# The last two feed-forward tiles as seven block products, two of them held over, and the modulation jobs distributed anew

## The chip, the cores and the metric

The kernel runs on one core of a Trainium2 chip. The metric is the device time of one execution in microseconds (us), lower is better. A run is one execution; a profiled execution also leaves a trace.

## The reference

One inference step of a two-layer backbone over 640 tokens (512 latent, 128 context) of width 1024. Each layer is a half-step SwiGLU feed-forward, a token mixer (layer 0 a Fourier mixer, layer 1 a 16-head attention), and another half-step feed-forward. Each sub-layer has a norm before and after it, with shift, scale and gate from a modulation of the conditioning vectors.

```python
def _half_ffn(x, m, k, g_pre, g_post, w1, w2):
    h = _rmsnorm(x, g_pre) * (1 + m[:, 3 * k + 1, None]) + m[:, 3 * k, None]
    gate, up = jnp.split(h @ w1, 2, axis=-1)          # w1: 1024 x 5632
    y = (jax.nn.silu(gate) * up) @ w2                 # w2: 2816 x 1024
    return x + 0.5 * m[:, 3 * k + 2, None] * _rmsnorm(y, g_post)

def _modulation(cond, w_mod, b_mod):                  # w_mod: 1024 x 9216 per layer
    return (jax.nn.silu(cond) @ w_mod + b_mod).reshape(cond.shape[0], 9, D_MODEL)
```

All of it is float32.

## The kernel before

**Layout.** Activations lie transposed: 1024 channels as 8 chunks of 128 partitions, the 640 tokens along the free axis in two halves of 320. Every fp32 product is made of three float32r matmuls (`mm3`, L203 to L208): a high part times a high part, high times low, low times high. `split` (L200 ACT, L201 DVE) makes the two parts of an activation, L190 (ACT) and L191 (DVE) those of a weight.

**Units.** All weights pass through one list of units of 128x1024 (`list_units`). `unit(i)` sends units up to i + 3: a 512 KB DMA on SP's queue into one of 4 raw buffers (`raw`), then L190 and L191 into one of 6 pairs of weight buffers, or, for a "block", into two blocks of a ring of 20 (`ring`), which also holds activations.

**Sub-layers.** n = 0 to 5: feed-forward, Fourier, feed-forward, feed-forward, attention, feed-forward. In the text "layers 0, 2, 3, 5" are the feed-forward ones by this n. Each ends half 0 with `boundary`, which starts a chain of steps for that half: the post norm, the residual, the next pre norm (`post`, `pre`). The chain of half 0 runs on DVE and ACT while PE still works on half 1; the next sub-layer's first matmuls need its result.

**A feed-forward layer** has 22 f tiles of 128 (NF = 22). A tile needs gate and up, each over 8 chunks and 2 halves. Tiles 0 to 3 are done plainly. Tiles 4 to 19 (`FAST`) go through `w1_fast`, a Strassen-Winograd scheme: gate and up against the lower and upper 4 chunks and the two halves of the tokens make a 2x2 block product, done as seven products of 4 chunks each, on sums of weights (L175 to L183, units gate, sums, up, all) and sums of activations (`combine`). Products go to banks x, y, z, w; DVE and ACT add between them (L587 to L609); `hidden` splits the result into g[f]. The second products (`w2`) run by slices of f tiles; slice s adds to `y` through a seed (L621) and a copy back (L633). Slices 0 to 3 are woven between the fast tiles, 16 steps each. Tiles 20 and 21 are done plainly by `late` after the fast ones: both for half 0, then 20 for half 1; 21 for half 1 comes after half 0's second products of the last slice, as cover for half 0's chain. `late` reuses the first 4 chunks' sum of half 0 for half 1, which it copies out of the half-summed bank (L539).

**Modulation jobs.** 128 jobs (`behind`): each loads 512 KB of w_mod into a raw buffer and does two multiply-and-sum operations on DVE (`gemv`, L336). `BEHIND` spreads them over a feed-forward layer's second products; the Fourier and attention code calls `behind` at places of its own. The whole order of instructions on each engine is fixed when the program is built, by a list scheduler that goes by priority and by its own estimate of what is ready; `high_priority` moves an instruction forward there.

Of the kernel before, what the change touches and what calls it, by code (L numbers as in the profile page):

```python
# [42 lines left out]
FAST = range(4, NF - 2)  # L43
BEHIND = (28, 20, 28, 28, 24, 0)
# [64 lines left out]
class Kernel:  # L109
    def __init__(self, ctx, tc, io, subs=6):  # L110
# [23 lines left out]
        self.fast = {}  # L134
# [29 lines left out]
    def send(self, kind, src):  # L164


        nc, two, one = self.nc, slice(512, UNIT), slice(0, 512)
# [23 lines left out]
        nc.vector.tensor_tensor(lo, raw[:, at], hi.bitcast(F32), op=ALU.subtract)  # L191
        return hi, lo
# [288 lines left out]
    def ffn(self, layer, which, base, boundary):  # L481
# [12 lines left out]
        def w1(fs, half):  # L494
# [4 lines left out]
            if fs[0] >= NF - 2:  # L499
                pss = [late(fs[0], j, half) for j in range(2)]  # L500
            elif len(fs) == 1:
# [5 lines left out]
            for i, f in enumerate(fs):  # L507
                gate, up = pss[2 * i], pss[2 * i + 1]
                s, v = self.temp("left"), self.temp("right")
                with self.tc.high_priority():  # L510
                    if f in kept and half:
                        for j, (to, ps) in enumerate(((s, gate), (v, up))):
                            nc.vector.tensor_tensor(to[:, :HALF], ps[:, :HALF], kept[f][j], op=ALU.add)
                        nc.scalar.activation(s[:, :HALF], s[:, :HALF], AF.Silu)
                        nc.vector.tensor_tensor(v[:, :HALF], v[:, :HALF], s[:, :HALF], op=ALU.mult)
                    else:
                        nc.scalar.activation(s[:, :HALF], gate[:, :HALF], AF.Silu)
                        nc.vector.tensor_tensor(v[:, :HALF], up[:, :HALF], s[:, :HALF], op=ALU.mult)  # L518
# [4 lines left out]
        def late(f, j, half):  # L523


            if f not in kept:
                if not kept:
                    kept["room"] = quad(self.ring(F32))
                a = 2 * (f - NF + 2)
                kept[f] = [kept["room"][:, a + i, :] for i in range(2)]  # L530
            w = self.unit(base + self.w1_at[f] + j)
            ps = self.bank()
            for k in range(NCH):
                x = part(1, k) if half and k < 4 else self.h.chunk(k, half)
                self.mm3(ps[:, :HALF], w[0][:, k * P : (k + 1) * P], w[1][:, k * P : (k + 1) * P], *x,
                         k == 0, k == NCH - 1 or (k == 3 and not half), k > 3 and not half)
                if k == 3 and not half:
                    with self.tc.high_priority():
                        nc.scalar.activation(kept[f][j], ps[:, :HALF], AF.Copy)  # L539
            return ps  # L540
# [27 lines left out]

        def w1_fast(f):
            g[f] = self.ring(F32R).rearrange("p (a t) -> p a t", a=2)  # L570
            u = base + self.w1_at[f]

            def product(ps, unit, at, x, start):
                w = self.unit(u + unit)
                for k in range(4):
                    a = at + k * P
                    self.mm3(ps[:, :HALF], w[0][:, a : a + P], w[1][:, a : a + P], *x(k), start and k == 0, k == 3, not start)

            tt = nc.vector.tensor_tensor
            a, q = (self.temp("left")[:, :HALF] for _ in range(2))  # L580
            s, v = (self.temp("right")[:, :HALF] for _ in range(2))
            px, py, pz, pw = self.bank(), self.bank("score"), self.bank(), self.bank()
# [694 lines left out]
```

## Time and profile before

| what | value |
|---|---|
| median of 3 runs | 2336.14 us (2333.36 to 2336.28) |
| profiled execution | 2334.2 us |
| its span, first to last instruction | 2332.4 us |
| mean granted TensorE clock | 0.993 |
| PE matmul / weight load busy | 98% / 95% |
| DVE / ACT busy | 72% / 54% |
| matmuls | 15756 |
| DMA moved | 278.13 MB, mean 119 GB/s |

A busy share is an average over stages with different limits; matmuls are pipelined, so the durations of single ones overlap, and how many start in a stretch says more than their sum. DVE is VectorE, ACT ScalarE, PE TensorE, SP the engine that issues the DMAs. A name such as `main<-ring,hi` reads: output tile from input tiles, buffer numbers left out.

### The profile page before, as it was taken

The page shows a single profiled execution, that of the slowest core. Times are in us where ns is not written, and L with a number is a line of the kernel's source. Part 1 is how long each engine was busy: PE and PEld are TensorE (multiplying, and loading weights), DVE is VectorE, ACT ScalarE, POOL GpSimd, SP SyncE. Part 2 cuts the span into 40 slices and gives each one's busy share as a digit, 9 for nine tenths or more (in the row PEclk, how much of TensorE's full clock was granted, in tenths as well). Part 3 has the DMA queues.
Part 4 walks back from the last instruction along what each step waited for, and adds up shares of the span by engine and source line. Part 5 has one row for each costly group of instructions (what it writes and reads, how often), then busy time and mean ns, then how long its engine had stood idle before and what let it go on. Part 6 is the DMA issues. An engine that isn't in the chain of part 4 may idle for free.

```text
span 2332.4 us, 39397 instructions
## 1 busy us (share of the span) xinstructions
PE 2278.2 (98%) x15756; PEld 2225.2 (95%) x15756; DVE 1686.6 (72%) x2934; ACT 1270.9 (54%) x2448; POOL 45.4 (2%) x64
## 2 busy tenths in 40 slices
PE   6999999998999999999999999999999999999997
PEld 4999999997999999999999999998888899999997
DVE  4878877389788877847878887378877485765553
ACT  4445545564653545556545555567767664545554
POOL 0000000000000000000000000010000000000000
PEclk9999999999999999999999999999999999999998
DMA  8234434334423433443234434224543212221241
GB/s 300 82 115 139 145 118 136 109 103 153 146 99 112 152 109 127 136 154 109 82 125 129 145 118 144 101 81 149 162 135 106 86 73 82 93 89 64 82 136 46
DMA packets 80280, 278.13 MB, mean 119 GB/s; under 512 B 8800, under 2 KB 15200, under 8 KB 79968
## 3 DMA queue, kind: packets, MB, share of 16 engines
q1 hardware_dynamic: 79824, 275.29, 36.1%
q8 instruction: 123, 2.02, 0.4%
q14 instruction: 61, 0.50, 0.1%
q10 hardware_dynamic: 272, 0.33, 0.0%
HBM read 264.04 MB, written 11.53 MB: 118 GB/s over the span
## 4 chain that ended last, share of the span: by engine, by line
PE 88%; DVE 5%; ACT 3%; DMA 3%; issue 1%; POOL 0%; SPq 0%; DVEq 0%; ACTq 0%; POOLq 0%
PE main L206 25%; PE main L208 25%; PE main L207 25%; PE score L206 3%; PE score L208 3%; PE score L207 3%; DVE junk L336 1%; PE sum L1108 1%; PE turn L1092 1%; PE sum L419 1%; DVE lo L191 1%; ACT hi L190 1%; PE score L1066 1%; DMA first<-in_w_mod_k 1%; DMA raw<-in_w_mod_t 1%
## 5 line engine op out<-in xcount | busy, mean ns | idle before, releaser
L206 PE MATMUL main<-ring,hi 128*128 128x320 f32 x3872 | 1204.5, 312 | 3.9 <-ACT ring L200 2.9
L208 PE MATMUL main<-ring,lo 128*128 128x320 f32 x3872 | 1198.0, 310 | 1.6 <-DVE lo L191 1.6
L207 PE MATMUL main<-ring,hi 128*128 128x320 f32 x3872 | 1198.9, 310 | 0.2 <-DVE ring L201 0.2
L206 PEld LDWEIGHTS main<-ring,hi 128*128 128x128 f32 x3872 | 727.7, 188 | 10.0 <-ACT ring L200 3.8
L208 PEld LDWEIGHTS main<-ring,lo 128*128 128x128 f32 x3872 | 727.6, 188 | 2.2 <-DVE lo L191 1.9
L207 PEld LDWEIGHTS main<-ring,hi 128*128 128x128 f32 x3872 | 728.1, 188 | 1.4 <-DVE ring L201 0.9
L190 ACT ACTIVATE hi<-raw 128x1024 fp32r<-128x1024 f32 (+1 forms) x358 | 350.3, 981 | 457.7 <-PE main L207 384.2
L191 DVE TENSOR_TENSOR lo<-raw,hi 128x1024 fp32r<-128x1024 f32 (+1 forms) x358 | 402.6, 1126 | 153.7 <-ACT hi L190 152.5
L336 DVE SCALAR_TENSOR_TENSOR junk<-raw,wide 128x1024 bf16<-128x1024 f32 x256 | 312.4, 1220 | 21.2 <-DMA raw<-in_w_mod_t 18.6
L633 ACT ACTIVATE y<-main 128x320 f32<-128x320 f32 x320 | 138.5, 433 | 172.3 <-PE main L208 170.9
L372 DVE TENSOR_TENSOR total<-total,square 128x640 f32<-128x640 f32 x71 | 58.3, 823 | 108.0 <-ACT square L371 106.1
L621 ACT ACTIVATE main<-y 128x320 f32<-128x320 f32 x256 | 111.9, 439 | 27.2 <-DVE left L607 10.5
L206 PE MATMUL score<-ring,hi 128*128 128x320 f32 x384 | 118.8, 309 | 0.0
L207 PE MATMUL score<-ring,hi 128*128 128x320 f32 x384 | 118.7, 309 | 0.0
L208 PE MATMUL score<-ring,lo 128*128 128x320 f32 x384 | 118.7, 309 | 0.0
L191 DVE TENSOR_TENSOR lo<-sums,hi 128x1024 fp32r<-128x1024 f32 x64 | 78.1, 1221 | 51.1 <-ACT hi L190 51.1
L206 PE MATMUL main<-ring,ring 128*128 128x320 f32 x352 | 110.5, 315 | 0.0
L208 PE MATMUL main<-ring,ring 128*128 128x320 f32 x352 | 108.9, 309 | 0.0
L207 PE MATMUL main<-ring,ring 128*128 128x320 f32 x352 | 108.7, 309 | 0.0
L190 ACT ACTIVATE hi<-sums 128x1024 fp32r<-128x1024 f32 x64 | 67.9, 1061 | 26.4 <-PE main L207 20.5
L200 ACT ACTIVATE ring<-right 128x320 fp32r<-128x320 f32 x112 | 51.6, 467 | 50.6 <-DVE right L518 40.6
L593 DVE TENSOR_TENSOR left<-left,main 128x320 f32<-128x320 f32 x64 | 31.2, 487 | 60.6 <-PE main L208 60.6
(181 smaller groups left out, 2676.1 us busy)
## 6 DMA issues: line engine op xcount, KB each, us to landing
raw<-in_w SPq DMA_DIRECT2D x264, 512.0 KB, 3.6
raw<-in_w_mod_t SPq DMA_DIRECT2D x128, 512.0 KB, 3.7
raw<-in_qkv SPq DMA_DIRECT2D x26, 512.0 KB, 3.7
first<-in_w_mod_k SPq DMA_DIRECT2D x16, 512.0 KB, 8.7
spill<-ring SPq DMA_DIRECT2D x12, 640.0 KB, 3.6
ring<-spill SPq DMA_DIRECT2D x12, 640.0 KB, 4.8
raw<-in_bias SPq DMA_DIRECT2D x16, 448.0 KB, 3.7
raw<-in_four_in SPq DMA_DIRECT2D x8, 512.0 KB, 3.5
```

Source lines behind the costliest of these rows:

```text
L190: nc.scalar.activation(hi, raw[:, at], AF.Copy)
L191: nc.vector.tensor_tensor(lo, raw[:, at], hi.bitcast(F32), op=ALU.subtract)
L200: self.nc.scalar.activation(hi, src, AF.Copy)
L206: mm(out, whi, xhi, start=start, stop=False)
L207: mm(out, whi, xlo, start=False, stop=False)
L208: self.latest = mm(out, wlo, xhi, start=False, stop=stop)
L336: last = self.nc.vector.scalar_tensor_tensor(out=self.junk, in0=raw, scalar=1.0, in1=self.wide[:, cond, :], op0=ALU.mult, op1=ALU.mult, ac ...
L372: nc.vector.tensor_tensor(acc, acc, sq, op=ALU.add)
L419: self.spread = nc.tensor.matmul(ps[:, t : t + P], col[:, j : j + 1].to_broadcast([P, P]), self.ident, start=True, stop=True)
L593: tt(a, q, z, op=ALU.subtract)
L621: nc.scalar.activation(ps[:, :HALF], self.y[:, m, lo:hi], AF.Copy)
L633: nc.scalar.activation(self.y[:, m, lo:hi], ps[:, :HALF], AF.Copy)
```

## The change

`FAST` now reaches to tile 21, and `late` goes. Tiles 20 and 21 (`LATE`) run as five of their seven products in `w1_fast`, which give half 0 whole; the partial sums a and q of half 1 stay in two temporaries. The other two products (`one`, `two`, on bank w) are `tail`, and both tails stand between half 0's and half 1's second products of the last slice. Their weights are one more unit, "mix", whose 1024 columns are the sum that was "up" and the difference that was "all"; it is built in place in the raw tile by "u2" and stays in that raw buffer until "mix" splits it into ring blocks. The jobs per sub-layer n go from 28, 20, 28, 28, 24, 0 to 36, 12, 28, 32, 12, 8: in a feed-forward layer they now also follow half 0's second products of the last slice (but for n = 5); in the Fourier layer three follow each fold of half 1, none lies among the groups of `positions`, and six stay in the output projection; in attention every third step has one.

```diff
-FAST = range(4, NF - 2)
-BEHIND = (28, 20, 28, 28, 24, 0)
+FAST = range(4, NF)
+LATE = (NF - 2, NF - 1)
+BEHIND = (36, 12, 28, 32, 12, 8)
...
-        elif kind == "up":
+        elif kind in ("up", "u2"):
             raw = self.fast["up"]
+            at = at if kind == "up" else two
+        elif kind == "mix":
+            raw = self.mixed.pop(0)
...
-        if kind == "block":
+        if kind in ("block", "mix"):
             hi, lo = (self.ring(F32R)[:, :n] for _ in range(2))
...
+        if kind == "u2":
+            nc.vector.scalar_tensor_tensor(out=raw[:, two], in0=self.fast["sums"][:, two], scalar=-1.0,
+                                           in1=self.fast["gate"][:, two], op0=ALU.mult, op1=ALU.subtract)
+            self.mixed.append(raw)
...
         def w1_fast(f):
...
-            product(pw, 2, 0, lambda k: part(1, k), True)
-            with high():
-                tt(a, a, w, op=ALU.add)
-            product(px, 0, 512, lambda k: self.h.chunk(4 + k, 0), False)
+            if not late:
+                w = one(f, a, 2)
+            product(f, x, 0, 512, lambda k: self.h.chunk(4 + k, 0), False)
             with high():
                 nc.scalar.activation(s, x, AF.Silu)
-            product(pz, 2, 512, lambda k: part(4, k), False)
+            product(f, z, 2, 0 if late else 512, lambda k: part(4, k), False)
             with high():
                 tt(v, q, z, op=ALU.subtract)
                 tt(v, v, s, op=ALU.mult)
                 hidden(f, v, 0)
-            product(pw, 3, 0, lambda k: self.h.chunk(4 + k, 1), False)
+            if late:
+                kept[f] = a, q
+            else:
+                two(f, a, q, w, 3, 0)
+
+        def one(f, a, unit):
+            w = self.bank()[:, :HALF]
+            product(f, w, unit, 0, lambda k: part(1, k), True)
+            with high():
+                tt(a, a, w, op=ALU.add)
+            return w
+
+        def two(f, a, q, w, unit, at):
+            product(f, w, unit, at, lambda k: self.h.chunk(4 + k, 1), False)
             with high():
                 nc.vector.scalar_tensor_tensor(out=q, in0=w, scalar=-1.0, in1=q, op0=ALU.mult, op1=ALU.subtract)
                 nc.scalar.activation(q, q, AF.Silu)
                 tt(a, a, q, op=ALU.mult)
                 hidden(f, a, 1)
+
+        def tail(f):
+            a, q = kept[f]
+            mix = self.mix_at[f] - self.w1_at[f]
+            two(f, a, q, one(f, a, mix), mix, 512)
...
-                if a[0] < len(SLICES) - 1:
+                if a[0] < len(SLICES) - 1 or half == 0:
                     passed += 1
-                    due = BEHIND[n] * passed // (2 * NCH * (len(SLICES) - 1))
+                    due = min(BEHIND[n], BEHIND[n] * passed // (2 * NCH * (len(SLICES) - 1) + (NCH if n < 5 else 0)))
...
-        a, b = NF - 2, NF - 1
-        plan += [("w1", (a,), 0), ("w1", (b,), 0), ("w1", (a,), 1), ("x", None, None)]
+        plan += [("x", None, None)]
         for half in (0, 1):
             if half == 1:
-                plan += [("w1", (b,), half)]
+                plan += [("tail", f, None) for f in LATE]
             plan += [("w2", (due, m), half) for m in range(NCH)]
             plan += [("end", None, half)]
...
-                self.ffn_units += [("gate", v, 0), ("sums", v, 1), ("up", None, None), ("all", None, None)]
+                self.ffn_units += [("gate", v, 0), ("sums", v, 1)]
+                self.ffn_units += [(kind, None, None) for kind in (("u2",) if v in LATE else ("up", "all"))]
+            elif op == "tail":
+                self.mix_at[v] = len(self.ffn_units)
+                self.ffn_units += [("mix", None, None)]
...
                 if half:
                     fold(m0, nc.vector)
-                self.behind(2)
+                    self.behind(3)
...
             positions(g)
-            if g < 6:
-                self.behind()
...
-            if n < 35 and (n % 5 < 3 or n in (3, 8, 13)):
+            if n < 35 and n % 3 == 0:
                 parts.append(self.behind)
```

## Rows read from the trace of the kernel before

**Rows 1.** The page: busy time of each engine (part 1).

```profile
PE 2278.2 (98%) x15756; PEld 2225.2 (95%) x15756; DVE 1686.6 (72%) x2934; ACT 1270.9 (54%) x2448; POOL 45.4 (2%) x64
```

**Rows 2.** Busy time by stretch, feed-forward stretches; columns in the first line.

```profile
core 0: us, PE busy (x) PEld busy (x) DVE busy (x) ACT busy (x) POOL busy (x), PEclk, DMA share, GB/s
160.00:200.00 40.00, 40.00 (x275) 40.00 (x274) 34.24 (x61) 21.95 (x39) 0.00 (x0) 1.00 0.40 132
2000.00:2040.00 40.00, 40.00 (x274) 40.00 (x274) 26.39 (x41) 23.36 (x44) 0.00 (x0) 1.00 0.30 98
```

**Rows 3.** Busy time by stretch, the last two f tiles, layer 0.

```profile
394.00:436.00 42.00, 41.66 (x281) 40.99 (x280) 22.70 (x34) 20.61 (x36) 0.00 (x0) 1.00 0.62 204
436.00:456.00 20.00, 20.00 (x139) 20.00 (x138) 2.96 (x4) 12.03 (x24) 0.00 (x0) 1.00 0.05 17
```

**Rows 4.** Busy time by stretch, the Fourier layer's groups and their end.

```profile
550.00:580.00 30.00, 21.81 (x166) 19.80 (x167) 29.63 (x75) 14.77 (x33) 0.00 (x0) 0.91 0.32 102
575.00:580.00 5.00, 3.06 (x15) 2.77 (x15) 5.00 (x12) 1.33 (x4) 0.00 (x0) 0.50 0.43 142
```

**Rows 5.** Busy time by stretch, attention: the sum of six stretches, 1600 to 1840.

```profile
sum 240.00, PE 233.07 PEld 207.72 DVE 180.72 ACT 177.60 POOL 8.81; mean PE 38.85 PEld 34.62 DVE 30.12 ACT 29.60 POOL 1.47
```

**Rows 6.** Busy time by stretch, from half 0's end to half 1's, layer 0.

```profile
455.00:483.50 28.50, 28.50 (x200) 28.31 (x199) 21.85 (x33) 21.15 (x46) 1.70 (x2) 1.00 0.26 82
```

**Rows 7.** Timeline of DVE: start, duration (us); next layer's first low part.

```profile
481.67 0.82 DVE L201 TENSOR_TENSOR ring<-y,ring 128x640 fp32r<-128x640 f32 x1
```

**Rows 8.** Groups by line, 361 to 410: count, busy us, mean ns, idle before.

```profile
L191 DVE TENSOR_TENSOR lo<-raw,hi 128x1024 fp32r<-128x1024 f32 x9 | 11.0, 1222 | 3.7 <-ACT hi L190 3.7
L190 ACT ACTIVATE hi<-raw 128x1024 fp32r<-128x1024 f32 x9 | 9.5, 1061 | 13.8 <-PE main L207 9.9 <-DMA raw<-in_w 3.0 <-ACT right L599 0.9
...
L176 DVE TENSOR_TENSOR raw<-raw 128x512 f32<-128x512 f32 x2 | 1.4, 692 | 0.1
...
L607 DVE SCALAR_TENSOR_TENSOR left<-main,left 128x320 f32<-128x320 f32 x2 | 1.0, 484 | 0.0
```

**Rows 9.** Timeline, tile 19's SiLU in half 1; tile 20's multiply and low part.

```profile
411.35 0.47 ACT L608 ACTIVATE left<-left 128x320 f32<-128x320 f32 x1 [0.38 <-DVE left L607]
...
417.99 0.49 DVE L518 TENSOR_TENSOR right<-main,left 128x320 f32<-128x320 f32 x1 [2.06 <-PE main L208]
419.02 0.49 DVE L201 TENSOR_TENSOR ring<-right,ring 128x320 fp32r<-128x320 f32 x1 [0.54 <-ACT ring L200]
```

**Rows 10.** Line 539, copies of a half-summed bank: durations, who waited.

```profile
L539 ACT ACTIVATE ring<-main x16: 413/434/438, 413.6 to 2257.2; 128x320 f32<-128x320 f32 x16
...
  PEld main L206: 3.6, 12
  PE main L206: 0.8, 3
```

**Rows 11.** DMA issues by line: count, KB each, median us to landing.

```profile
raw<-in_w SPq DMA_DIRECT2D x264, 512.0 KB, 3.6
...
ring<-spill SPq DMA_DIRECT2D x12, 640.0 KB, 4.8
```

**Rows 12.** Line 336 (a job's gemv), last layer: DVE busy (count), clock, DMA.

```profile
1850.00:2290.00 440.00, 0.00 (x0) 1.00 0.26 87
```

**Rows 13.** Timeline of DVE, one Fourier group, from L855 to L855.

```profile
560.69 0.33 DVE L855 SCALAR_TENSOR_TENSOR ring<-main,col,ring 128x128 fp32r<-128x128 f32 x1
560.95 1.21 DVE L336 SCALAR_TENSOR_TENSOR junk<-raw,wide 128x1024 bf16<-128x1024 f32 x1
...
562.69 1.21 DVE L336 SCALAR_TENSOR_TENSOR junk<-raw,wide 128x1024 bf16<-128x1024 f32 x1
...
565.23 0.33 DVE L855 SCALAR_TENSOR_TENSOR ring<-main,col,ring 128x128 fp32r<-128x128 f32 x1
```

**Rows 14.** Waits, 1560 to 1845: us in total, times, longest.

```profile
PEld turn L1092 <- ACT right L1094: 10.3, 22, 1.4
...
PE turn L1092 <- ACT right L1094: 5.0, 11, 1.2
```

More of the change, by code (lines that the diff above doesn't have):

```diff
@@ L498, in w1 @@
             pss = []
-            if fs[0] >= NF - 2:
-                pss = [late(fs[0], j, half) for j in range(2)]
-            elif len(fs) == 1:
+            if len(fs) == 1:
                 for j in range(2):
@@ L510, in w1 @@
                 with self.tc.high_priority():
[L511 to L518, printed above, removed]
+                    nc.scalar.activation(s[:, :HALF], gate[:, :HALF], AF.Silu)
+                    nc.vector.tensor_tensor(v[:, :HALF], up[:, :HALF], s[:, :HALF], op=ALU.mult)
                     hidden(f, v, half)
@@ L521, in w1 @@
                     self.later.pop()()
[L523 to L540, printed above, removed]
         def part(i, k):
@@ L567, in combine, with product @@
                 self.split(sums[i][0][:, k : k + 2, :], sums[i][1][:, k : k + 2, :], to)
+        high, tt = self.tc.high_priority, nc.vector.tensor_tensor
+        def product(f, ps, unit, at, x, start):
+            w = self.unit(base + self.w1_at[f] + unit)
+            for k in range(4):
+                a = at + k * P
+                self.mm3(ps, w[0][:, a : a + P], w[1][:, a : a + P], *x(k), start and k == 0, k == 3, not start)
         def w1_fast(f):
             g[f] = self.ring(F32R).rearrange("p (a t) -> p a t", a=2)
-            u = base + self.w1_at[f]
@@ L573, in product @@
[L573 to L579, printed above, removed]
+            late = f in LATE
             a, q = (self.temp("left")[:, :HALF] for _ in range(2))
             s, v = (self.temp("right")[:, :HALF] for _ in range(2))
-            px, py, pz, pw = self.bank(), self.bank("score"), self.bank(), self.bank()
@@ L583, in w1_fast @@
-            x, y, z, w = (ps[:, :HALF] for ps in (px, py, pz, pw))
-            high = self.tc.high_priority
-            product(px, 0, 0, lambda k: self.h.chunk(k, 0), True)
+            x, y, z = (self.bank(kind)[:, :HALF] for kind in ("main", "score", "main"))
+            product(f, x, 0, 0, lambda k: self.h.chunk(k, 0), True)
             with high():
                 nc.scalar.activation(a, x, AF.Copy)
-            product(py, 1, 512, lambda k: part(2, k), True)
+            product(f, y, 1, 512, lambda k: part(2, k), True)
@@ L589, in w1_fast @@
             with high():
                 tt(q, y, a, op=ALU.subtract)
-            product(pz, 1, 0, lambda k: part(3, k), True)
+            product(f, z, 1, 0, lambda k: part(3, k), True)
             with high():
                 tt(a, q, z, op=ALU.subtract)
-            product(pw, 2, 0, lambda k: part(1, k), True)
-            with high():
-                tt(a, a, w, op=ALU.add)
-            product(px, 0, 512, lambda k: self.h.chunk(4 + k, 0), False)
+            if not late:
+                w = one(f, a, 2)
@@ L721, in list_units @@
                         elif op == "w1":
-                            self.units.append(("block" if v in (3, NF - 1) else "plain", io["w1"][i, sub // 2, v, j]))
+                            self.units.append(("block" if v == 3 else "plain", io["w1"][i, sub // 2, v, j]))
                         else:
```

6 lines of the change are left out of this document (4 added, 2 removed).

## The prediction

> **What bounds the kernel now.** I read the page's totals first, then the busy table in stretches of 40 us, then the waits inside the stretches where TensorE (PE) isn't full, and last the queues of the engines that feed it. The totals [rows 1] put matmuls at 98% of the span and VectorE (DVE) at 72%. In the feed-forward layers PE is full for hundreds of us: 40.00 of 40 us, 274.5 matmuls, in the densest stretch beside 34.24 us of DVE [rows 2]. That gives 40 / 274.5 = 0.1457 us for one 128x128x320 matmul, and there a removed matmul is worth its whole time. PE isn't full in three places: the last two f tiles of a feed-forward layer, a little [rows 3]; the groups of the Fourier layer, where DVE is busy 29.63 of 30 us and PE 21.81 [rows 4]; and the attention layer [rows 5].
>
> **The products.** Two f tiles in plain form are 2 tiles x 2 (gate, up) x 8 k x 2 halves x 3 matmuls = 192. As seven block products they are 2 x 7 x 4 x 3 = 168. 24 matmuls fewer in each of four layers: 96 x 0.1457 = 14.0 us off a full PE. 120 of the 168 come before half 0's second products (144 before the change) and 48 after them (48 before), so what covers half 0's norm chain stays 48 + 144 matmuls. That chain has its first chunk's low part at 481.67 + 0.82 = 482.5 us, while PE is busy without a gap up to 483.5 [rows 6, 7]: about 1 us of room.
>
> **New work on DVE and ACT.** Each late f tile is split as gate 1024, sums 1024, u2 512 and mix 1024 columns instead of 2048: 1536 columns more, 1.5 x 1.06 = 1.6 us of ACT and 1.5 x 1.22 = 1.8 us of DVE, and four 512-wide sums or differences of 0.69 = 2.8 us of DVE [rows 8]. For two tiles that is about 9 us of DVE, beside 4 more modulation jobs of 2.4 us in half 0's second products in layers 0, 2 and 3. Now DVE works 22.70 of 42 us and then 2.96 of 20 in this place [rows 3]: 25.7 + 9 + 9.8 = 44.5 of 62 - 3.5 us. The sum fits, so I charge no time for the amount, only for the order. Four places, each per layer:
> (a) Half 0. Tile 21 now ends with a product, and the second products need its result as their sixth tile, 5 x 3 x 0.1457 = 2.2 us later. Behind the product stand a subtraction (0.5), then multiply, high part and low part: multiply to low part takes from 417.99 to 419.02 + 0.49, 1.5 us [rows 9]. 2.0 us and the hand-over against 2.2: nothing if DVE is free, 1.2 if a 1024-wide split stands in the way. I take 0.3.
> (b) Half 1, behind the second tail: a negating subtraction 0.48 [rows 8], SiLU 0.47 [rows 9], then the same 1.5, so 2.5 and hand-overs, 0.3 to 0.5 late; up to 1.7 if an operation of the norm chain goes first. Taken: 0.5.
> (c) In a tail, product six is read by DVE out of the bank that product seven adds to, so PE must wait for that read unless other matmuls stand between. Nearest row: the old code copies a half-summed bank in the same way, 16 times, and PE waited 0.8 us for all 16 (its weight loads 3.6) [rows 10]: 0.05 each where the order leaves room. The other end is a read with nothing between, 0.49 and two hand-overs, about 0.9. Two tails a layer: 0.1 to 1.8; taken 0.4, less the 0.2 of the copies that go.
> (d) Load buffers. There are four; the raw tiles of both late f tiles stay in two of them from u2 to mix, so the six second-product units and two of the jobs must pass through the other two. One pass takes 3.6 us landing [rows 11] + 1.06 high + 1.22 low [rows 8] = 5.9. Eight through two buffers: 4 x 5.9 = 23.6 us, from about 1 us into tile 21's products (60 x 0.1457 = 8.7 us long) to the use of the sixth unit, 40 x 3 x 0.1457 = 17.5 us into the second products, 26.2 in all. Room of 1.6 us. Each us of landing beyond that room takes 4 us, and the four reloads of x (640 KB, landing 4.8 [rows 11]) now crowd into this stretch. At 4.8 the layer would lose 3.2. I take 0.6 for layers 0, 2, 3; layer 5 has no jobs here and takes 0.
> Sum: 0.3 + 0.5 + 0.2 + 0.6 = 1.6 in three layers, 1.0 in the last: 5.8. Bounds: -0.8 (only the copies go) to some 28 (1.2 + 1.7 + 1.8 + 3.2 in each of three layers, 4.7 in the fourth). Feed-forward net: 14.0 - 5.8 = 8.2 gained.
>
> On (c), the Trainium skill's "TensorE: Matmul & The Clock Gate", section "Part 2: What happens when you issue a matmul", speaks against the change: only weight loads are pulled ahead, "the MATMULs themselves stay in program order". By it alone the two products of a tail stand still at the read, which is rival 2. The row of the sixteen copies disagrees only if the written order put other matmuls between, which no row here names.
>
> **Modulation.** Jobs per layer go from 28, 20, 28, 28, 24, 0 to 36, 12, 28, 32, 12, 8. Layer 0's first four slices get 32 instead of 28: 9.8 us of DVE over some 300 us, 1.3 per 40, where the densest row has 34.24 [rows 2]. PE's cover holds until DVE is full; cost 0, and if the jobs bunch, some 2 us. Layer 5 gets 8 where DVE works 26.39 of 40 [rows 2] and had none [rows 12]: 0.
> Fourier: the six jobs among the groups go. A group now takes 565.23 - 560.69 = 4.54 us, with two 1.21 us gemv operations in it [rows 13]; without them DVE needs 2.1 to 2.2, and PE's own 21.81 / (30 / 4.54) = 3.3 us sets the pace. PE's idle 8.2 us of the 30 can go. The granted clock is 0.50 in the last 5 of them, behind the gaps [rows 4], that is 1.2 instead of 2.4 GHz: half of 3.06 busy us more, 9.7 in all. Against this stand six jobs behind the projections of half 1 (four stood there): two more, 4.9 us of DVE, run on into the first groups, and PE's slack over DVE there is about 1.1 a group, so some 2.7 are lost. Net 7.0. Ends: 9.7, and 9.7 - 7.3 = 2.4 if the three jobs behind the second fold stand in front of the first group's splits. The four jobs that leave half 0's projections free DVE where PE loses under 1 us: 0.
> Attention: 24 jobs to 12, 29 us less of DVE's 180.72 in 240 [rows 5]. But PE waits there for ACT copies (5.0 us) [rows 14], which a job delays only through what ACT waits for. Bounds 0 to 7 (7 is what PE isn't busy there); taken 1.5, near the lower end, as the row names ACT.
> Weight loads wait 10.3 us for those copies [rows 14]; if half of that goes with the jobs, attention gives 5, the figure of the high rival.
> By the Trainium skill's "Perfetto Trace Analysis", section "Identifying the Most-Contended Engine", weight-load time, not matmul time, measures PE's headroom: 207.72 of 240 instead of 233.07 [rows 5]. By it there is room for more than 5; no row here says that DVE stands behind it.
>
> **Sum.** 8.2 + 7.0 + 1.5 = 16.7. The profiled execution took 2334.2 us (span 2332.4 and 1.8 around it), 1.9 below the median of the runs shown, 2336.14. 2334.2 - 16.7 = 2317.5; I write 2318, as the runs lie a little above the profile.
>
> **Rivals.**
> 1. Everything is hidden: 14.0 - 0.5, Fourier 9.7, attention 5: 2334.2 - 28.2 = 2306. For it: PE lost only 0.34 us in the whole stretch of the old late tiles [rows 3]. Against it: DVE has twice the work there. Chance 0.2.
> 2. The tails stand still: 0.9 at each of 8 reads instead of 0.2, and (b) at 1.2: 5.6 + 2.8 more, 2326. For it: the two products of a tail are written one behind the other. Against: the copies' 0.05. Chance 0.14.
> 3. Slower: the load buffers. If a landing takes 5.9 us in half 0's second products, eight passes take 4 x 8.2 + 1 = 33.8 us, 7.6 late in each of layers 0, 2, 3; with (d) at 0 the rest gains 18.5, so about here the sum passes +0.2%. At 6.5 us: 9.9 x 3 = 29.8, 2345. For it: 6 units, jobs and 2.6 MB of x in 20 us where the DMA engines now carry nearly nothing [rows 3]. Against: x lands in 4.8 even now, with loads in front of it. Chance 0.07.
> 4. Nothing much moves: landings of 5 us (4 late in three layers, 10 more than summed) and the Fourier jobs only shifted (2.4): 2332. Chance 0.08.
>
> **Numbers.** The forecast has 0.51, in 2311 to 2324. A measurement of this kernel can tell about 0.2% (4.7 us) from no change: below 2331.4 is faster. Forecast, rivals 1 and 2 and a little of 4 give 0.86 for faster, 0.07 for the same, 0.07 for slower. The range takes in rival 1's time and rival 2's and leaves out the worst of 1, the upper part of 4 and 3: 2305 to 2329.
>
> **What would show it.** 15660 matmuls, 96 fewer, if no records are missing. In the stretch of the last two f tiles: PE gaps of 0.3 to 0.6 at the low part of the last tile (a, b), at the tail's read (c); and gaps at a second-product unit's high or low part whose ACT operation waited for a DMA (d). In the Fourier groups: a period near 3.3 us, the clock at full, DVE below 25 of 30. In attention DVE lower, PE's wait for ACT copies nearly as before. The prediction is wrong if PE's waits in the late tiles exceed 3.5 us a layer, if the six jobs turn up among the Fourier groups, or if PE falls behind in layer 0's slices.

## The result, and the profile after

The change takes 2321.2 us (median of 4 runs, 2319.2 to 2323.81) against 2336.21 (4 runs, 2333.36 to 2336.65): ratio 0.9939, 95% interval 0.9922 to 0.9956, some 15 us less. The profiled execution took 2319.2 us, span 2317.4; the one before took 2334.2. So profile against profile gives 15.0, where 16.7 was forecast.

The page's totals of the kernel after (before: [rows 1]):

```profile
PE 2260.0 (98%) x15660; PEld 2209.5 (95%) x15660; DVE 1731.6 (75%) x3006; ACT 1275.8 (55%) x2456; POOL 46.5 (2%) x64
```

There are 96 matmuls fewer. Line numbers have shifted: the three matmuls are now L215 to L217 (were L206 to L208), a weight's high and low part L195 and L196 (L190, L191), an activation's L209 and L210 (L200, L201), a job's gemv L345 (L336).

Busy time by stretch, after: three stretches of the last two f tiles and half 0's end in layer 0 (columns as in [rows 2]; they answer to [rows 3, 6]), the Fourier groups, and their end [rows 4]:

```profile
394.00:436.00 42.00, 40.25 (x274) 39.91 (x273) 28.20 (x46) 19.84 (x35) 0.00 (x0) 1.00 0.35 111
436.00:456.00 20.00, 20.00 (x139) 20.00 (x138) 15.32 (x23) 13.94 (x27) 0.00 (x0) 1.00 0.80 295
455.00:483.50 28.50, 28.24 (x196) 27.54 (x195) 22.92 (x38) 20.57 (x46) 2.61 (x2) 1.00 0.27 88
540.00:570.00 30.00, 29.19 (x235) 26.39 (x235) 26.30 (x62) 18.14 (x47) 0.00 (x0) 1.00 0.31 95
565.00:570.00 5.00, 5.00 (x45) 4.71 (x44) 3.70 (x12) 3.03 (x8) 0.00 (x0) 1.00 0.00 0
```

The reader is to see two things. In the Fourier groups PE now does 235 matmuls in 30 us instead of 166, and the granted clock stays at 1.00 where it had been 0.50. In the first row PE loses 1.75 us, in one single gap, where it had lost 0.34 [rows 3].

Where the whole span went is read from marks. The span is cut where the first fast tile's subtraction (L571, before L590) starts in each feed-forward layer. In us, each kernel's profile less the profile of before; the kernels in the rows are those of the experiments. Each row is one execution: the change and its control in experiment 4, which differ only in how the conditioning rows are kept, are 2.1 us apart in layer 3 with attention and up to 0.9 in the other columns, so small entries say little:

| kernel | start | layer 0 and Fourier | layer 2 | layer 3 and attention | layer 5 | sum |
|---|---|---|---|---|---|---|
| the change | +0.6 | -11.4 | +0.8 | -1.9 | -3.1 | -15.0 |
| products alone | +0.1 | -0.3 | -1.9 | -0.8 | -3.3 | -6.2 |
| jobs alone | +1.2 | -11.1 | +0.1 | -3.1 | -0.7 | -13.5 |
| jobs alone, none in last slice | +1.3 | -11.6 | 0.0 | -1.7 | -1.3 | -13.2 |
| change, none in last slice | +1.1 | -12.4 | -1.8 | -4.1 | -2.9 | -20.0 |
| change, five buffers | +1.9 | -11.9 | -2.3 | -2.4 | -4.4 | -19.1 |
| both of these | +2.1 | -13.1 | -3.4 | -3.3 | -4.4 | -22.0 |

In the change itself, layer 2 has 24 matmuls less (3.5 us) and is 0.8 us longer. PE is full in the fast stretches of these kernels (297.4 to 297.6 us from the first fast tile to tile 19; with five buffers 296.8 in layers 0, 2 and 3, where the first mark itself falls 0.8 later), so what is lost is lost between tile 19 and the next layer. The stretch from tile 19 of layer 2 to layer 3, first of before, then of after:

```profile
1001.27:1147.69 146.42, 145.81 (x997) 144.26 (x996) 97.73 (x149) 85.14 (x159) 4.29 (x4) 1.00 0.33 112
```

```profile
990.46:1137.65 147.19, 143.09 (x973) 140.74 (x972) 115.54 (x179) 87.49 (x161) 4.31 (x4) 1.00 0.39 133
```

Weight loads were idle 146.42 - 144.26 = 2.16 us and are now idle 147.19 - 140.74 = 6.45. The 4.29 more is just the 3.5 that went plus the 0.8 that came. PE waits in it for two kinds of thing, here as weight-load rows of the timeline (start, duration, and in brackets the idle time and what ended it), after:

```profile
1021.88 0.30 PEld L215 LDWEIGHTS main<-ring,hi 128*128 128x128 f32 x2 [1.73 <-ACT ring L209]
...
1066.08 0.74 PEld L428 LDWEIGHTS sum<-ident,col 128*128 128x128 f32 x6 [0.53 <-POOL col L423]
1078.42 0.74 PEld L428 LDWEIGHTS sum<-ident,col 128*128 128x128 f32 x6 [0.97 <-POOL col L423]
1101.17 0.74 PEld L428 LDWEIGHTS sum<-ident,col 128*128 128x128 f32 x6 [0.97 <-POOL col L423]
1105.60 0.58 PEld L215 LDWEIGHTS main<-ring,hi 128*128 128x128 f32 x4 [1.12 <-ACT ring L209]
```

The first is the sixth tile of half 0's second products, waiting for tile 21. The others are the norm chains of the two halves. Both had to be explained.

**The wait at the sixth tile.** Three queues in layer 0, after (start, duration, what the engine waited for), DVE and ACT, then PE:

```profile
427.99 1.23 DVE L196 TENSOR_TENSOR lo<-raw,hi 128x1024 fp32r<-128x1024 f32 x1 [2.81 <-ACT hi L195]
429.14 0.48 DVE L582 TENSOR_TENSOR right<-left,main 128x320 f32<-128x320 f32 x1
430.91 1.23 DVE L196 TENSOR_TENSOR lo<-raw,hi 128x1024 fp32r<-128x1024 f32 x1 [1.30 <-ACT hi L195]
432.06 0.48 DVE L583 TENSOR_TENSOR right<-right,right 128x320 f32<-128x320 f32 x1
```

```profile
429.82 1.06 ACT L195 ACTIVATE hi<-raw 128x1024 fp32r<-128x1024 f32 x1 [1.53 <-DMA raw<-in_w]
...
432.57 0.47 ACT L209 ACTIVATE ring<-right 128x320 fp32r<-128x320 f32 x1 [1.36 <-DVE right L583]
```

```profile
433.10 0.56 PE L215 MATMUL main<-ring,hi 128*128 128x320 f32 x2 [1.75 <-ACT ring L209]
```

Read it backwards. PE waits for the high part of tile 21 (L209), that for the multiply (L583). The multiply's operands were there from 429.6, after the subtraction (L582), but between the two stands the low part of a weight unit (L196). It waits for its high part (L195), which waits 1.53 us for its DMA. SP's queue shows that load:

```profile
424.81 0.33 SPq L156 DMA_DIRECT2D raw<-in_w  x1
```

SP had waited 1.1 us for the low part of an earlier unit, which ended on DVE at 423.57 + 1.22 = 424.79 and freed its raw buffer. The load landed some 5.0 us later, where the median of all units is 3.6. PE waits at this place in all four layers, 1.75, 1.47, 1.41 and 1.16 us, each time with a unit's low part in front of the multiply. In layers 2 and 3 that unit's high part had waited 1.47 and 1.17 us for its DMA; in layer 5 only 0.23 (the unit before it 1.08), so there the 1.22 us of the low part itself are most of the delay.

### The profile page after: what moved, and what is told of

The parts are those of the page before. It is cut to its first block, busy times and chain, and to the rows that moved or that the text cites. A ratio compares the mean times of both kernels' runs of the same rounds, so it can differ in the third digit from the quotient of the medians.

```text
span 2317.4 us, 39267 instructions
## 1 busy us (share of the span) xinstructions
PE 2260.0 (98%) x15660; PEld 2209.5 (95%) x15660; DVE 1731.6 (75%) x3006; ACT 1275.8 (55%) x2456; POOL 46.5 (2%) x64
## 4 chain that ended last, share of the span: by engine, by line
PE 87%; DVE 4%; ACT 4%; DMA 3%; issue 1%; POOL 0%; SPq 0%; DVEq 0%; ACTq 0%; POOLq 0%
PE main L215 25%; PE main L217 25%; PE main L216 25%; PE score L215 3%; PE score L217 3%; PE score L216 3%; DMA raw<-in_w 2%; DVE lo L196 1%; PE sum L428 1%; PE turn L1093 1%; ACT hi L195 1%; PE sum L1109 1%; DMA first<-in_w_mod_k 1%; PE sum L419 1%; PE score L1067 1%
## 5 line engine op out<-in xcount | busy, mean ns | idle before, releaser
L215 PE MATMUL main<-ring,hi 128*128 128x320 f32 x3872 | 1203.7, 312 | 9.6 <-ACT ring L209 9.6
L217 PE MATMUL main<-ring,lo 128*128 128x320 f32 x3872 | 1195.3, 309 | 1.6 <-DVE lo L196 1.6
L215 PEld LDWEIGHTS main<-ring,hi 128*128 128x128 f32 x3872 | 726.7, 188 | 16.5 <-ACT ring L209 11.8
L217 PEld LDWEIGHTS main<-ring,lo 128*128 128x128 f32 x3872 | 726.8, 188 | 1.9 <-DVE lo L196 1.9
L195 ACT ACTIVATE hi<-raw 128x1024 fp32r<-128x1024 f32 (+1 forms) x366 | 355.4, 974 | 445.0 <-PE main L216 372.0
L196 DVE TENSOR_TENSOR lo<-raw,hi 128x1024 fp32r<-128x1024 f32 (+1 forms) x366 | 408.2, 1118 | 139.6 <-ACT hi L195 138.5
L345 DVE SCALAR_TENSOR_TENSOR junk<-raw,wide 128x1024 bf16<-128x1024 f32 x256 | 312.6, 1221 | 16.3 <-DMA raw<-in_w_mod_t 13.7
L196 DVE TENSOR_TENSOR lo<-sums,hi 128x1024 fp32r<-128x1024 f32 x72 | 88.0, 1222 | 60.7 <-ACT hi L195 60.7
L215 PE MATMUL score<-ring,hi 128*128 128x320 f32 x416 | 128.6, 309 | 0.0
L216 PE MATMUL score<-ring,hi 128*128 128x320 f32 x416 | 128.5, 309 | 0.0
L217 PE MATMUL score<-ring,lo 128*128 128x320 f32 x416 | 128.5, 309 | 0.0
L195 ACT ACTIVATE hi<-sums 128x1024 fp32r<-128x1024 f32 x72 | 76.3, 1060 | 28.7 <-PE main L216 17.4
L215 PE MATMUL main<-ring,ring 128*128 128x320 f32 x288 | 90.1, 313 | 0.0
L216 PE MATMUL main<-ring,ring 128*128 128x320 f32 x288 | 89.2, 310 | 0.0
L217 PE MATMUL main<-ring,ring 128*128 128x320 f32 x288 | 89.2, 310 | 0.0
L216 PEld LDWEIGHTS score<-ring,hi 128*128 128x128 f32 x416 | 78.1, 188 | 0.0
```

What stands on the lines that cost most here:

```text
L195: nc.scalar.activation(hi, raw[:, at], AF.Copy)
L215: mm(out, whi, xhi, start=start, stop=False)
L216: mm(out, whi, xlo, start=False, stop=False)
L217: self.latest = mm(out, wlo, xhi, start=False, stop=stop)
L345: last = self.nc.vector.scalar_tensor_tensor(out=self.junk, in0=raw, scalar=1.0, in1=self.wide[:, cond, :], op0=ALU.mult, op1=ALU.mult, ac ...
```

## The experiments

After the two traces the theory was: the products are worth their 14 us, but two raw tiles held over starve the load buffers, and what is late then blocks DVE's and ACT's queues; the jobs are worth more than forecast. Its rivals: the order in DVE's queue alone, the tails themselves, or the jobs that now run on beside the tails. Each kernel ran beside the kernel before on the same chip; the medians of the latter were 2334.5 to 2335.4 (2336.2 beside the change), so differences between kernels that did not run side by side carry some 1 to 2 us. The numbers after a median are the interval of the ratio.

**1. The products alone.** The jobs stand as before.

```diff
-BEHIND = (36, 12, 28, 32, 12, 8)
+BEHIND = (28, 20, 28, 28, 24, 0)
...
-                if a[0] < len(SLICES) - 1 or half == 0:
+                if a[0] < len(SLICES) - 1:
...
+            if g < 6:
+                self.behind()
...
```

> The products alone: the changed kernel with the modulation jobs at their old places (28, 20, 28, 28, 24, 0). Theory A (the 14 us of products are mostly lost again in the late tiles and behind them, and the Fourier layer's gain comes from the jobs): the Fourier groups keep their 8 us of PE idle time and the half clock; about -5 us against the kernel before, 2331. Rival B (the Fourier layer gains because its norm chain starts earlier): about -13 us, 2323. If the four jobs in half 0's second products cause the loss in the late tiles (rival C), the stall in front of the sixth tile, 1.7 + 1.5 + 1.4 + 1.2 us, goes here: about -10 us and small gaps.

Measured: 2330.5 us (0.9970 to 0.9988), 4.8 below the kernel before beside it. Theory A holds in the main: from 550 to 580 us PE still idles 5.9 of 30 us, and the granted clock in the last 5 is 0.64 (0.50 before [rows 4]). Rival C does not: the wait at the sixth tile is there without any new job, 1.65, 1.40, 1.95 and 1.44 us in the four layers. So the products bring 5 of their 14 us.

**2. The jobs alone.** The old `late` tiles, the new distribution; the edit is against the kernel before.

```diff
-BEHIND = (28, 20, 28, 28, 24, 0)
+BEHIND = (36, 12, 28, 32, 12, 8)
...
-                if a[0] < len(SLICES) - 1:
+                if a[0] < len(SLICES) - 1 or half == 0:
...
-            if g < 6:
-                self.behind()
...
```

> The jobs alone: the kernel before with the new distribution 36, 12, 28, 32, 12, 8. Theory A: the Fourier groups lose their PE idle time (8.5 us between 520 and 600 us to under 1) and the half clock; attention and the feed-forward layers as before: -9 to -11 us, 2326. Rival B: no change there, within 2 us of before. If the new jobs themselves slow what follows the feed-forward layers, layers 2 and 3 end later than before here as well, and the sum is nearer -5.

Measured: 2321.6 us (0.9928 to 0.9953). That is 13.7 less, more than the 9 to 11 expected and nearly the whole gain of the change; on top of it the products bring 0.4, which is within the scatter between kernels that did not run side by side.

**3. The multiply on GpSimd.** If only the order in DVE's queue were at fault, taking the multiply of tile 21 out of that queue should cure the wait.

```diff
-                tt(v, v, s, op=ALU.mult)
+                (nc.gpsimd.tensor_tensor if f == NF - 1 else tt)(v, v, s, op=ALU.mult)
```

> The changed kernel with one instruction of tile 21's half 0 moved: the multiply behind the last product on GpSimd instead of VectorE, once per feed-forward layer. Theory A (the multiply is ready but stands behind a weight's low part in VectorE's queue, which waits for its high part and that for its DMA): PE's wait in front of the sixth tile falls from 1.2 to 1.7 us to 0.4 or less in each layer, with about 0.8 us for the multiply itself: -4 us against the change, 2317. Rival D (the second-product units come too late in any case): PE then waits for the low part of a unit instead, and the time stays at 2321.

Measured: 2323.4 us (0.9934 to 0.9959), no gain. PE waits 1.19, 1.06, 2.07 and 2.65 us at that place. In layer 3 ACT's queue shows one reason (timeline of this kernel):

```profile
1464.45 1.06 ACT L195 ACTIVATE hi<-raw 128x1024 fp32r<-128x1024 f32 x1 [2.32 <-DMA raw<-in_w]
1465.41 0.42 ACT L619 ACTIVATE main<-y 128x320 f32<-128x320 f32 x1
1465.77 0.45 ACT L209 ACTIVATE ring<-right 128x320 fp32r<-128x320 f32 x1
```

The tile's own high part now stands behind a weight's high part that waits 2.32 us for its DMA: the block has moved from one queue to the next. In layers 0 and 2 this costs only 0.3 to 0.4 us; there the subtraction in front of the multiply starts late, directly behind a low part that had waited 2.74 and 1.91 us for its high part, and the multiply takes 0.88 us instead of 0.48. In layer 5 PE waits for the multiply itself, 1.94 us long. So DVE's order at the multiply alone is not the cause; that the late loads are it is an inference, which the next experiment tests.

**4. Five load buffers.** The late tiles hold two of four. The room for a fifth comes from the conditioning rows, which are kept in bfloat16 here, so the modulation is less exact.

```diff
-NRAW = 4
+NRAW = 5
...
-        self.wide = keep.tile([P, 2, D], F32, name="wide")
+        self.wide = keep.tile([P, 2, D], mybir.dt.bfloat16, name="wide")
...
+        rows = [self.raw_tile(io["cond_rows"][i : i + 1].to_broadcast([P, D])) for i in range(2)]
...
```

> The changed kernel with five load buffers instead of four; for their room the conditioning rows are kept in bfloat16, so the modulation is less exact. Theory A': the two raw tiles held over leave two buffers, and the DMA of a second-product unit starts late; with three the unit's high part no longer waits for its DMA, the low part no longer blocks the multiply, and PE's wait in front of the sixth tile goes: -4 to -6 us against the change, 2316. Rival E: the DMA is late for another reason (the x reloads, SP's order), the high part still waits for it, and the time stays within 1.5 us of the change.

Measured: 2315.4 us (0.9902 to 0.9929), 5.8 below the change. The waits of PE for ACT's high parts in the whole run, of the change and then of this kernel (us, times, longest):

```profile
PE main L215 <- ACT ring L209: 10.4, 7, 2.9
```

```profile
PE main L215 <- ACT ring L209: 6.5, 4, 3.2
```

About 2.9 us of either was there before the change, in one wait. At the sixth tile the expected cure came in part: 2.2 us are left of 5.8, 1.06 in layer 0 and 1.10 in layer 3. What stands in front of the multiply there is now an operation of a job (DVE, layer 0):

```profile
430.01 0.48 DVE L582 TENSOR_TENSOR right<-left,main 128x320 f32<-128x320 f32 x1
430.41 1.22 DVE L345 SCALAR_TENSOR_TENSOR junk<-raw,wide 128x1024 bf16<-128x1024 f32 x1
...
431.55 0.49 DVE L583 TENSOR_TENSOR right<-right,right 128x320 f32<-128x320 f32 x1
```

The control keeps four buffers and has only the rows in bfloat16:

```diff
-NRAW = 5
+NRAW = 4
```

> A control: the change with the conditioning rows in bfloat16, but still four load buffers. If the fifth buffer was what gained 6 us, this is the change's own time, 2320 to 2322.5, with its waits of 1.2 to 1.75 us at the sixth tile of half 0's second products. If the rows were (a modulation job reads half the bytes), it is 2315 to 2317 and a job's operation is shorter than 1.21 us.

Measured: 2321.9 us (0.9932 to 0.9957), the change's own time. The fifth buffer was it.

**5. No job beside the tails.** From layer 2's gaps above: with the products alone that stretch had fallen by 1.9, in the change it rose by 0.8. What differs there is the jobs in half 0's second products of the last slice. The kernel has all products, the same number of jobs in each sub-layer, but in the first four slices only.

```diff
-                if a[0] < len(SLICES) - 1 or half == 0:
+                if a[0] < len(SLICES) - 1:
-                    due = min(BEHIND[n], BEHIND[n] * passed // (2 * NCH * (len(SLICES) - 1) + (NCH if n < 5 else 0)))
+                    due = BEHIND[n] * passed // (2 * NCH * (len(SLICES) - 1))
```

> The change with one edit undone: no modulation job stands in half 0's second products of the last slice; the same 36, 12, 28, 32, 12, 8 jobs go over the first four slices. Theory B (the products' gain is lost because these jobs run on beside the tails and push half 1's norm chain some 2 us back in layers 0, 2 and 3): the stretch from the last fast tile of layer 2 to the first one of layer 3 falls by about 2 us against the kernel before, as with the products alone (1.9), where the change had it 0.8 above; about 2315 to 2317 in all. Rival B1 (the gain is lost in the tails and their load buffers whatever the jobs do): 2320 to 2322. Rival B2 (the jobs cost PE the same wherever they stand; nine a slice fill VectorE in layer 0): the fast stretch of layer 0 grows from 297.6 by 2 us or more, and the sum is 2322 or above.

Measured: 2314.3 us (0.9899 to 0.9926), 6.9 below the change (7.6 below the control of experiment 4, which ran beside it); layer 2's stretch fell by 1.8. Theory B holds. The sixth tile is not where the gain comes from: PE still waits 2.17, 1.00, 1.34 and 1.45 us there. It comes from the norm chains: the waits of the weight loads of the norm's matmuls (the column sums, L419, and their spread, L428), whole run, in the change and then in this kernel ("issue" is idle time whose release the profile does not show):

```profile
PEld sum L419 <- issue: 11.0, 9, 6.5
PEld sum L428 <- POOL col L423: 10.6, 13, 1.9
```

```profile
PEld sum L419 <- issue: 8.5, 5, 4.9
...
PEld sum L428 <- POOL col L423: 6.9, 7, 1.9
```

With 0.6 us in a smaller row that is 21.6 us against 16.0; the kernel before had 15.5. One place where the delay arises can be read from DVE's queue in half 0's chain, at the sums of squares of its pre norm. First the change, then this kernel (tile 19 stands 0.49 us later in it):

```profile
469.43 1.22 DVE L196 TENSOR_TENSOR lo<-raw,hi 128x1024 fp32r<-128x1024 f32 x1
470.57 0.82 DVE L381 TENSOR_TENSOR total<-total,square 128x640 f32<-128x640 f32 x1
471.70 1.23 DVE L196 TENSOR_TENSOR lo<-raw,hi 128x1024 fp32r<-128x1024 f32 x1 [0.30 <-ACT hi L195]
472.84 1.75 DVE L381 TENSOR_TENSOR total<-total,square 128x640 f32<-128x640 f32 x2
474.62 0.49 DVE L411 TENSOR_TENSOR total<-total 128x320 f32<-128x320 f32 x1
```

```profile
469.42 1.22 DVE L196 TENSOR_TENSOR lo<-raw,hi 128x1024 fp32r<-128x1024 f32 x1
470.55 1.75 DVE L381 TENSOR_TENSOR total<-total,square 128x640 f32<-128x640 f32 x2
472.63 0.82 DVE L381 TENSOR_TENSOR total<-total,square 128x640 f32<-128x640 f32 x1 [0.34 <-ACT square L380]
473.49 0.49 DVE L411 TENSOR_TENSOR total<-total 128x320 f32<-128x320 f32 x1
473.94 1.23 DVE L196 TENSOR_TENSOR lo<-raw,hi 128x1024 fp32r<-128x1024 f32 x1
```

In the change a third weight unit's low part (471.70) stands between the sums of squares. Without jobs there it comes behind the total (473.94), and the total starts at 473.49 - 0.49 = 473.0 on the change's clock instead of 474.62. The same order, with the same 0.30 us wait for a high part, is in layers 2 and 3 of the change (1060.47 and 1504.91). Half 1's chain, which follows on DVE, is later by more: its second total in layer 2, in the change and then in this kernel (tile 19 stands 0.50 us earlier in it):

```profile
1098.49 0.48 DVE L411 TENSOR_TENSOR total<-total 128x320 f32<-128x320 f32 x1
```

```profile
1093.51 0.48 DVE L411 TENSOR_TENSOR total<-total 128x320 f32<-128x320 f32 x1
```

That is 4.5 us. Not all of it is traced to the one unit: in layer 0 the next sub-layer's first low part of half 0 starts no earlier here, although its total does. Why the list scheduler puts that unit earlier when jobs stand in front was not followed further.

**6. Are those jobs dear by themselves?** The same removal in experiment 2's kernel, without the products.

```diff
-                if a[0] < len(SLICES) - 1 or half == 0:
+                if a[0] < len(SLICES) - 1:
...
```

> The jobs' new distribution without the products (the kernel before in its feed-forward layers), and without jobs in half 0's second products of the last slice. If the jobs there cost only beside the tails (the tails' chain on VectorE is what they delay), their removal brings nothing here: 2320.5 to 2322, as with the jobs alone (2321.6). If they cost the same beside the old late tiles, this is 2315 to 2317 by itself, and the products bring next to nothing on top of it either (2314.3).

Measured: 2320.8 us (0.9922 to 0.9949), against 2321.6 with them. They cost under 1 us beside the old late tiles and 6.9 beside the tails. It is the pair that is dear.

**7. Both cures.** Experiments 4 and 5 in one.

> The last kernel with five load buffers as well (the conditioning rows in bfloat16 to make room). If jobs and load buffers are two separate causes, their gains of about 5 and 6 us add: 2310 to 2313. If the fifth buffer only helps because the jobs no longer crowd out the six units, it brings nothing more here: 2315 to 2317, as each alone.

Measured: 2311.8 us (0.9885 to 0.9915), the fastest of all: 22.8 below the kernel before beside it (2334.5). The gains add in part, 2.5 of the buffer's 5.8, and the waits tell why: both edits cure the same ones. The norm's weight loads wait 17.1 us in all with five buffers, 16.0 without the jobs, 17.1 with both, and 21.6 in the change. Only both together clear the sixth tile: with five buffers alone an operation of a job stands in front of the multiply, without the jobs alone the low part of a unit. So beside five buffers the jobs cost 3.7 us (2315.4 to 2311.8), not 6.9. Here the queue of DVE at the sixth tile reads

```profile
428.93 0.48 DVE L582 TENSOR_TENSOR right<-left,main 128x320 f32<-128x320 f32 x1
429.52 0.49 DVE L583 TENSOR_TENSOR right<-right,right 128x320 f32<-128x320 f32 x1
429.93 1.22 DVE L196 TENSOR_TENSOR lo<-raw,hi 128x1024 fp32r<-128x1024 f32 x1
431.06 0.48 DVE L210 TENSOR_TENSOR ring<-right,ring 128x320 fp32r<-128x320 f32 x1
```

The multiply comes first; a weight load waits 0.15 us there for the low part, and PE itself in no layer.

**8. What the fifth buffer brings without the products.** In the kernel before, and in experiment 6's kernel; the edits are those of experiment 4.

> The kernel before with five load buffers (conditioning rows in bfloat16). If the buffer pays for what the change holds over, it brings little here: TensorE waited only 2.9 us for high parts in the whole run, so 2332 to 2335. If it helps any kernel of this kind (the first 100 us, the attention layer), the 6 us come here too: 2328 to 2330.

> The jobs' new distribution without the products, no jobs in the last slice, with five load buffers: the last kernel but one without its seven block products. It prices the products where neither the jobs beside the tails nor the load buffers hold them up (the kernel with them takes 2311.8). If the fifth buffer's 4.2 us in the kernel before came where the old jobs crowded (the Fourier groups), it gives nothing here: 2319.5 to 2321, and the products are worth 8 to 9 of their 14 us. If its gain adds, 2316 to 2317.5, and the products are worth 4 to 6 even then, so something else than jobs and buffers holds them up.

Measured: 2331.2 us (0.9975 to 0.9993), 4.2 below before, between the two guesses; and 2323.9 us (0.9936 to 0.9963), 3.1 above experiment 6. The second was forecast by neither theory. So a buffer neither simply adds nor pays nothing. That it does so by shifting the built order of the queues is likely but not shown. In the second kernel the loss lies in layer 0 and the Fourier layer (+3.3 us against experiment 6 by the marks). New gaps of weight loads stand there, in the norm chain and at the first Fourier groups (lines as in the kernel before):

```profile
510.80 0.74 PEld L419 LDWEIGHTS sum<-ident,col 128*128 128x128 f32 x6 [1.16 <-POOL col L414]
516.69 0.84 PEld L206 LDWEIGHTS main<-ring,hi 128*128 128x128 f32 x4 [0.54 <-ACT ring L200]
...
551.69 0.19 PEld L208 LDWEIGHTS main<-hi,ring 128*128 128x128 f32 x1 [1.00 <-DVE ring L201]
```

So what the products are worth depends on their surroundings: 4.8 us with the old jobs, 0.4 with the change's, 6.5 (2320.8 to 2314.3) with no job beside the tails, 12.1 (2323.9 to 2311.8) with that and five buffers. The last figure holds some of the 3.1 that the buffer costs without them.

**9. Nothing held over.** Both late tiles run all seven products before half 0's second products; what covers half 0's norm chain falls from 192 to 144 matmuls.

```diff
-LATE = (NF - 2, NF - 1)
+LATE = ()
```

> The change with no unit held over: both late tiles run as seven block products each before half 0's second products, so half 0's norm chain has 144 matmuls (21.0 us) of half 1 behind it instead of 192 (28.0 us). The prediction's account (about 1 us of room in 28): 6 us uncovered in layers 0, 2 and 3, less the 1.4 us of load-buffer waits that go in each: 14 us more than the change, 2333 to 2338. Rival (the tails delay half 1 as much as they cover of half 0): 2319 to 2323.

Measured: 2325.4 us (0.9949 to 0.9974), 4.2 above the change: neither the 14 of the prediction's account nor within the rival's 2319 to 2323. In layer 0 the chain lies bare as expected, in three gaps of weight loads (this kernel's timeline):

```profile
480.00 0.74 PEld L419 LDWEIGHTS sum<-mean,total 128*128 128x128 f32 x6 [0.53 <-PE main L217]
482.07 0.74 PEld L428 LDWEIGHTS sum<-ident,col 128*128 128x128 f32 x6 [1.33 <-POOL col L423]
487.11 0.77 PEld L215 LDWEIGHTS main<-ring,hi 128*128 128x128 f32 x3 [4.30 <-ACT ring L209]
```

Together 6.2 us, where 6 was expected, 5.7 in layer 2 and 6.1 in layer 3. But the waits of the change in the same places go: by the marks layer 0 with the Fourier layer is 7.7 us longer than in the change and layer 2 only 2.6, layer 3 with attention 0.9 shorter and layer 5 2.8 shorter. Holding over earns its cover and gives most of it back. Around the sixth tile it gives back 4.8 us (5.8 in the change, 1.0 here); how the rest divides between the held buffers and the order of the queues is not separated.

## Why the prediction came out, step by step

The time, 2321.2, lies within the forecast's own range, and within 3.2 of 2318. That it came so near is in part luck, two errors that cancel: the modulation brought 13.7 us alone where 8.5 was forecast, the feed-forward part 4.8 alone, and 0.4 on top of the jobs, where 8.2 was. None of the prediction's three signs of being wrong came: PE waits 1.2 to 1.8 us a layer at the sixth tile, no job stands among the later Fourier groups, and PE is full in layer 0's slices.

**Products.** The count and the gross 14.0 were right. In layer 5, where no next sub-layer waits for half 1, the products alone gave 3.3 of their 3.5.

**(a) Half 0, and (d) load buffers: the steps that failed.** "Nothing if DVE is free, 1.2 if a 1024-wide split stands in the way. I take 0.3." The split did stand in the way, in every layer. And (d) looked for the shortage at the sixth unit, eight passes on, with 1.6 us of room and none needed in layer 5; it showed at the end of tile 21, where a unit in the queue in front of the multiply waited for its DMA, and in layer 5, where no job passes and that unit was nearly in time, its low part was in the way by itself. The terms 0.3 and 0.6 belong together, and measure 1.16 to 1.75 a layer. The Trainium skill has the rule that makes this so ("TensorE: Matmul & The Clock Gate", section "Architectural detail: the array is 16× 32×32, not 1× 128×128"): ScalarE and VectorE take their queues strictly in order. The trace agrees: L583, ready at 429.6, starts at 432.06 behind L196. The reloads of x landed in 7.3 us (median, 4.8 before [rows 11]), but in layer 0 they were sent at 432.55, after the late load. A unit's median stayed at 3.6, and the load that mattered took 5.0.

**(b) Half 1.** 0.5 was charged behind the second tail. That place is on time: its low part starts at 464.70 and the weight load waits 0.18. The loss is later, in the norm chains of both halves, and with four buffers it comes with the jobs beside the tails: 6.9 us in all by the medians, 5.6 of them read as waits of the norm's weight loads. I had charged these jobs nothing but their share in (d), and the chains "about 1 us of room". This is the largest term missed, and it isn't a term of amount: DVE was 15.32 of 20 us busy in front of the tails and 22.92 of 28.5 behind.

**(c) The tail's read.** Taken 0.4, measured 0 in the change but for one weight load's 0.2 (0.7 in four, without jobs beside the tails). Rival 2 is wrong.

By the Trainium skill's rule on program order, named in the prediction and read on the order as written, both products of a tail would have stood still. No run breaks that rule; the order built here has other matmuls between the two (six in layer 0 of experiment 5), so the written order was not the queue's.

**Modulation.** In the slices nothing was lost: PE is full beside 35.81 of 40 us of DVE (nine jobs a slice, experiment 5, 360 to 400 us). The Fourier layer gave about 11 where 7.0 was taken. From tile 19 of layer 0 to layer 2, weight loads are idle 5.4 us in experiment 6's kernel (290.97 - 285.57) and were 15.2 (302.56 - 287.40): 9.8 from gaps, and 1.8 from the busy time, where the clock had been 0.50. The gaps and the clock were read rightly; wrong was the 2.7 set against them for jobs that run on into the first groups. Timeline of DVE, after, one job operation and then two groups, each by its L855 operation:

```profile
550.57 1.22 DVE L345 SCALAR_TENSOR_TENSOR junk<-raw,wide 128x1024 bf16<-128x1024 f32 x1
...
558.29 0.41 DVE L855 TENSOR_TENSOR y<-left,main 128x252 f32<-128x252 f32 x1
...
561.39 0.41 DVE L855 TENSOR_TENSOR y<-left,main 128x252 f32<-128x252 f32 x1
```

One operation ran on, and it is not what PE waited for: PE lost 0.8 us at the first group, up to 547.01, for a high part that ACT did behind a weight's high part, which had waited 0.84 us for its DMA. The period is 3.1 us, where 3.3 was forecast; DVE, at 26.30 of 30, is not below the 25 that I had named, but no longer sets the pace. Attention, with layer 3, gave 1.7 to 3.1 (jobs alone, two distributions; 1.5 forecast), no more than the 2.1 us by which two executions differ there. The row that I went by held: PE's wait for ACT's copies did not fall with the jobs ([rows 14] had 5.0):

```profile
PE turn L1093 <- ACT right L1095: 5.8, 13, 0.8
```

The Trainium skill's "Perfetto Trace Analysis", section "Identifying the Most-Contended Engine", wants headroom read from weight-load time. The trace agrees in layer 2: the idle time of weight loads accounts for the whole loss (4.29 us), that of matmuls (0.61 to 4.10) for 3.49.

**Rivals.** Rival 1 (all hidden, 2306) was not reached, even with both cures. Rivals 3 and 4 stood on landings of 5 us and more for all eight passes; a single load took that long in layer 0, and the median stayed at 3.6.

Left open: why the scheduler's order turns as it does, and why the first fast tile starts 0.6 to 2.1 us later than before in most of these kernels (0.8 of it, with five buffers, is the mark).

## What to carry to other kernels

Ask of each buffer that an edit holds longer not only whether the loads still fit on average, but which operation will wait for the late load, and what stands behind it in that in-order queue: here a 1.2 us split that nobody needed yet held up the one result that PE needed. Work that fills idle time costs under 1 us beside one neighbour and 7 us beside another, so two edits that are tried together should be tried apart and crossed; here that found 7 us, and a fifth buffer 2.5 more. In a kernel whose order a list scheduler writes, price a change by the order that comes out.

## What the runs showed that was not expected

One load buffer more made the kernel with the new jobs and without the products 3.1 us slower (2323.9 against 2320.8), and the kernel before 4.2 us faster. Moving a 128x320 multiply to GpSimd cost 0.88 us instead of 0.48, and 1.94 in one of four cases.
